# A hybrid decoder step on one core: retention's masked products one chunk later, one product for the new tokens' scores, the last group norm behind the next gate row, and token stores on ScalarE's queue

## Chip, cores and metric

One core of one Trainium2 chip runs the whole step as one program. The metric is device time in microseconds, from the host's view of one execution; the median of several runs counts. The profile is of one more execution, taken by the hardware profiler.

## What is computed

One step of a decoder layer for a prompt of 1024 tokens and for 8 sequences of 4 new tokens each, which have 1024 cached tokens behind them. Attention over the 256 best keys (chosen by an indexer) and retention (a linear recurrence in chunks of 128 tokens) run beside each other and are merged by gates. Of the reference, the parts that the change touches:

```python
def retention_chunk(state, q, k, v):
    ...
    scores = jnp.einsum('bihd,bjhd->bhij', q, k) * dmat
    out = jnp.einsum('bhij,bjhe->bihe', scores, v)
    ...
    out = out + jnp.einsum('bihd,bhde->bihe', q, state) * q_decay[None, :, :, None]
    ...
    new_state = (jnp.exp(lg * C)[None, :, None, None] * state
                 + jnp.einsum('bjhd,bjhe->bhde', k * k_decay[None, :, :, None], v))

def group_norm_heads(o):
    mu = jnp.mean(o, axis=-1, keepdims=True)
    var = jnp.mean(jnp.square(o - mu), axis=-1, keepdims=True)
    y = (o - mu) * lax.rsqrt(var + EPS)

def index_scores(qi, wi, ki):
    s = jnp.einsum('bqhd,bsd->bqhs', qi.astype(jnp.float32), ki.astype(jnp.float32))
    ...
    return jnp.einsum('bqhs,bqh->bqs', jax.nn.relu(s), w)
```

The step also returns the keys and values of all tokens, token by token.

## The kernel before

Activations are kept transposed, channels by tokens: 1056 tokens (1024 of the prompt, 32 new ones) in three chunks of 352 columns. A **row** of the projection is 128 output channels: for each chunk, 24 products of 128x128 weights (three terms for each of eight input tiles, lines 225 to 227) fill one PSUM bank `pj`, and ScalarE or VectorE copies the bank out. There are two such banks in the pool `psj`; while `third[0]` is set, every third chunk takes a bank `pj3` out of the retention's own pool. The weights of a row are loaded by SP (`ws`, L204), cast by ScalarE (`wh`, L210), and the remainder is subtracted by VectorE or GpSimd (`wl`, L211).

The program is written as one stream. A scheduler orders each engine's instructions by a timeline of its own, within the data's order and the `issue_after` limits that the code states; each engine then runs its list strictly in order. `last_on(engine)` is the last instruction that was written for an engine.

`retention` runs over four pairs of heads. For a pair, `pair` projects keys, queries, values and gates, rotates keys and queries, builds the eight chunk states (the scan L758, copied to `SD` by L760), and makes the scores (L766), which VectorE masks (L774). Between stands `rows`, a generator that projects a row of attention queries (`split_rows`): `next(rows)` makes one of its three chunks, casts it on ScalarE (L613) and subtracts the rest on VectorE (L616); after the third, four small copies take the new tokens' part (L619). After the first chunk come the state products (L784) and the masked-score products (L787), whose result is copied and transposed into `O` (L793 to L798). The group norm follows: mean on VectorE (L807, L808), centring on GpSimd (L810), Square on ScalarE (L812), variance and reciprocal root on VectorE (L814 to L817), scaling on GpSimd (L818), transposes on PE (L824). Then a gate row (`gates`, tanh on ScalarE, L880), the modulation's gate columns (`gate_rows`, products L218, copy L655, sum L659) and a second gate row.

In the last pair `new_tokens` runs ahead of the norm: scores of all new tokens' keys and queries (two products L847, one for each head, in two banks, masked by L851), output (L853), the products with the old states and the new states (L861, L863), the state update on VectorE (L867), and the old states' part of the output (L872 to L874). `third[0]` is cleared in it, because one of its banks is `pj3`.

VectorE has a second task over this stretch: the choice of the 256 best keys, whose passes (L1052 and lines up to 1135) fill its list; ScalarE counts signs for it (L1059).

Behind the retention come four key rows and four value rows. Each is turned into tokens (`to_tokens`, L678, copied to `tk` by L1179) and stored (L1181, L1183; the values once more to a scratch tensor, L1185). Between them stand the scores of the new queries against cached keys: SP loads gathered keys (`kv`, L1265), VectorE transposes them (`kt`, L1271), PE multiplies (L1250). SP issues in order, so a load stands behind a store that waits for its copy.

Early in the program the indexer's scores of the new tokens against cached keys pass through six ReLUs on ScalarE (L1026, L1028), then through the products L1032 on PE.

Of the kernel before, what the change touches and what calls it, by code (L numbers as in the profile page):

```python
# [8 lines left out]
F32 = mybir.dt.float32  # L9
# [4 lines left out]
OP = mybir.AluOpType  # L14
# [109 lines left out]
def _hybrid_step(ctx, tc, A, outs, dbg):  # L124
# [504 lines left out]
    def retention(gp):  # L629
        with ExitStack() as s3:  # L630
# [51 lines left out]
    def pair(rp, RC, O, SD, new, p, rows):  # L682
# [31 lines left out]
        for x, t in ((KN, kT), (QN, qT)):  # L714
            nc.gpsimd.tensor_copy(x[:, p], t[:, T:])
# [62 lines left out]

        end = next(rows)
# [21 lines left out]
        if p == 3:  # L801
            new_tokens(rp, RC, O, new, rows, vtok[:, 8], kd[:, 8])

        n, n8 = (18, 9) if p == 3 else (16, 8)
        o18 = O[:, :n8].rearrange("p t h e -> p (t h) e")
        mu = rp.tile([128, 18], F32, name="mu", bufs=1)[:, :n]
        nc.vector.tensor_reduce(mu, o18, op=OP.add, axis=AX.X)  # L807
        nc.vector.tensor_scalar(mu, mu, -1.0 / 64, None, op0=OP.mult)  # L808
        yc = o18
        nc.gpsimd.tensor_tensor(yc, o18, mu.unsqueeze(2).to_broadcast([128, n, 64]), op=OP.add)  # L810
        sq = big(rp, "tmp")[:, :n8].rearrange("p t (h e) -> p (t h) e", h=2)
        nc.scalar.activation(sq, yc, AF.Square)  # L812
        va = rp.tile([128, 18], F32, name="va", bufs=1)[:, :n]
        nc.vector.tensor_reduce(va, sq, op=OP.add, axis=AX.X)  # L814
        nc.vector.tensor_scalar(va, va, 1.0 / 64, EPS, op0=OP.mult, op1=OP.add)
        rs = rsqrt(rp, va, n, room=18)
        nc.vector.tensor_scalar(rs, rs, 0.5, None, op0=OP.mult)  # L817
        nc.gpsimd.tensor_tensor(yc, yc, rs.unsqueeze(2).to_broadcast([128, n, 64]), op=OP.mult)  # L818
        y2 = yc.rearrange("p (t h) e -> p t (h e)", h=2)
        yT = flat(big(rp, "tmp"))  # L820
        for g in (0, 1):
            p_ = pt()
            for j in range(4):
                nc.tensor.transpose(p_[:, 128 * j:128 * j + 128], y2[:, 4 * g + j], ident)  # L824
            sl = slice(512 * g, 512 * g + 512)
            normed[p] = nc.vector.scalar_tensor_tensor(yT[:, sl], p_, gT[:, p:p + 1], zsT[:, sl], op0=OP.mult, op1=OP.mult)
# [924 lines left out]
```

## Time and profile before

| | |
|---|---|
| time, median of 3 runs | 1049.01 us (1048.07 to 1051.84) |
| time of the profiled execution | 1049.86 us |
| its span, first to last instruction | 1048.2 us |
| mean granted clock of TensorE | 0.994 |
| ScalarE busy | 450.2 us |
| GpSimd busy | 223.9 us |
| DMA, mean over the span | 193 GB/s |

A profile names engines PE (matmul), PEld (weight load), DVE (VectorE), ACT (ScalarE), POOL (GpSimd) and SP (the queue that issues most transfers; SPq and ACTq mark the issuing of a transfer). Tiles are written `out<-in`. A row of a timeline gives start and duration in us, engine, line, operation, tiles, shape, and in brackets how long the engine stood idle before it and what ended that. A row of the waits gives engine, tile and line that waited, what ended the wait, us in total, times, and the longest.

### The profile page before, as it was taken

The page shows a single profiled execution, that of the slowest core. Times are in us where ns is not written, and L with a number is a line of the kernel's source. Part 1 is how long each engine was busy: PE and PEld are TensorE (multiplying, and loading weights), DVE is VectorE, ACT ScalarE, POOL GpSimd, SP SyncE. Part 2 cuts the span into 40 slices and gives each one's busy share as a digit, 9 for nine tenths or more (in the row PEclk, how much of TensorE's full clock was granted, in tenths as well). Part 3 has the DMA queues.
Part 4 walks back from the last instruction along what each step waited for, and adds up shares of the span by engine and source line. Part 5 has one row for each costly group of instructions (what it writes and reads, how often), then busy time and mean ns, then how long its engine had stood idle before and what let it go on. Part 6 is the DMA issues. An engine that isn't in the chain of part 4 may idle for free. (4 is left out here: it accounts for less than half of the span.)

```text
span 1048.2 us, 20021 instructions
## 1 busy us (share of the span) xinstructions
PE 1023.3 (98%) x7766; PEld 952.4 (91%) x7766; DVE 684.4 (65%) x1537; ACT 450.2 (43%) x926; POOL 223.9 (21%) x192
## 2 busy tenths in 40 slices
PE   7999999999999999999899999999999999999996
PEld 6899999999999999998799998778999999998776
DVE  6877369788977878989344443111367676586765
ACT  5685445554654555232233222122256576433111
POOL 0017436013320211120200021532033333000000
PEclk9999999999999999999899999999999999999998
DMA  9937676375445726664588788868867511656531
GB/s 303 282 81 198 190 224 176 104 225 155 143 150 165 194 63 221 173 144 144 172 307 291 262 261 299 285 217 297 276 228 232 203 68 32 210 178 224 186 106 61
DMA packets 183907, 202.53 MB, mean 193 GB/s; under 512 B 24308, under 2 KB 153348, under 8 KB 182724
## 3 DMA queue, kind: packets, MB, share of 16 engines
q1 hardware_dynamic: 171520, 175.07, 53.3%
q0 software_dynamic: 11776, 25.32, 7.6%
q8 instruction: 61, 1.00, 0.4%
q10 hardware_dynamic: 516, 0.86, 0.2%
q14 instruction: 34, 0.28, 0.1%
HBM read 156.11 MB, written 57.95 MB: 204 GB/s over the span
## 5 line engine op out<-in xcount | busy, mean ns | idle before, releaser
L225 PE MATMUL pj<-hh,wh 128*128 128x352 f32 (+1 forms) x1168 | 383.4, 328 | 1.1 <-ACT raw L880 0.8
L227 PE MATMUL pj<-hh,wl 128*128 128x352 f32 (+1 forms) x1168 | 377.2, 323 | 0.2 <-POOL wl L211 0.2
L226 PE MATMUL pj<-hl,wh 128*128 128x352 f32 (+1 forms) x1168 | 377.2, 323 | 0.0
L225 PEld LDWEIGHTS pj<-hh,wh 128*128 128x128 f32 x1168 | 219.9, 188 | 11.1 <-issue 6.8
L227 PEld LDWEIGHTS pj<-hh,wl 128*128 128x128 f32 x1168 | 219.9, 188 | 3.1 <-issue 2.5
L226 PEld LDWEIGHTS pj<-hl,wh 128*128 128x128 f32 x1168 | 220.3, 189 | 2.5 <-issue 2.1
L1052 DVE TENSOR_SCALAR_CACHE_REDUCE eq<-sc,cand 128x896 bf16<-128x896 f32 (+4 forms) x155 | 135.8, 876 | 2.8
L210 ACT CAST wh<-ws 128x1024 fp32r<-128x1024 f32 (+1 forms) x65 | 61.1, 941 | 125.6 <-PE pj L226 88.1
L211 POOL TENSOR_TENSOR wl<-ws,wh 128x1024 fp32r<-128x1024 f32 x18 | 43.7, 2428 | 224.4 <-ACT wh L210 224.2
L211 DVE TENSOR_TENSOR wl<-ws,wh 128x1024 fp32r<-128x1024 f32 (+1 forms) x47 | 54.5, 1161 | 47.1 <-ACT wh L210 47.0
L1436 POOL TENSOR_SCALAR lg<-lg,st 128x1024 f32<-128x1024 f32 (+7 forms) x64 | 47.3, 761 | 110.0 <-DVE st L1433 100.3
L1271 DVE STREAM_TRANSPOSE kt<-kv 128x1024 f32<-128x1024 f32 x32 | 38.7, 1234 | 43.5 <-DMA kv<-KG 43.2
L1428 ACT ACTIVATE lg<-lg,st 128x1024 f32<-128x1024 f32 (+7 forms) x64 | 49.5, 775 | 28.8 <-DVE st L1422 24.5
L1662 PE MATMUL pj<-woh,MH 128*128 128x512 f32 (+1 forms) x136 | 51.4, 378 | 0.0
L1663 PE MATMUL pj<-wol,MH 128*128 128x512 f32 (+1 forms) x136 | 51.2, 377 | 0.0
L1664 PE MATMUL pj<-woh,ML 128*128 128x512 f32 (+1 forms) x136 | 51.2, 377 | 0.0
L1241 POOL DMA_INDIRECT kv<-in_cache_v,idx x32 | 31.8, 994 | 57.8 <-PE sx L1305 40.2
L880 ACT ACTIVATE raw<-pj 128x352 f32<-128x352 f32 x48 | 21.8, 460 | 45.1 <-PE pj L227 42.5
L1679 ACT ACTIVATE u<-xo 128x512 f32<-128x512 f32 (+2 forms) x19 | 11.6, 609 | 67.0 <-DVE xo L1678 42.9
L1059 ACT ACTIVATE ra<-sc,cand 128x1024 bf16<-128x1024 f32 x31 | 35.6, 1149 | 6.2 <-DVE cand L1135 5.6
L1059 ACT ACTIVATE ra<-scs,cand 32x1056 bf16<-32x1056 f32 x31 | 36.4, 1175 | 0.8
L1422 DVE CUSTOM_DVE_ANT_0 lg<-x,bi 128x512 f32<-128x512 f32 (+3 forms) x64 | 35.3, 570 | 1.5 <-PE x L1421 1.1
(389 smaller groups left out, 1837.2 us busy)
## 6 DMA issues: line engine op xcount, KB each, us to landing
ws<-in_w_in SPq DMA_DIRECT2D x49, 512.0 KB
kv<-KG SPq DMA_DIRECT2D x32, 512.0 KB
KG<-in_cache_k SPq DMA_DIRECT2D x40, 256.0 KB
rot<-in_rot SPq DMA_DIRECT2D x8, 1056.0 KB
x<-in_w_ada SPq DMA_DIRECT2D x16, 512.0 KB
TG<-raw SPq DMA_DIRECT2D x15, 528.0 KB
KG<-in_cache_k POOLq DMA_DIRECT2D x24, 256.0 KB, 8.0
wst<-in_w_out SPq DMA_DIRECT2D x12, 512.0 KB
```

The costliest lines, as they stand in the source:

```text
L210: nc.scalar.copy(wh[:, :, :n], ws[:, :, :n])
L211: (nc.vector if k == 4 or len(order) % 3 else nc.gpsimd).tensor_sub(wl[:, :, :n], ws[:, :, :n], f32(wh[:, :, :n]))
L225: nc.tensor.matmul(p, wh[:, k], HH[k][:, sl], start=(k == 0), stop=False)
L226: nc.tensor.matmul(p, wh[:, k], HL[k][:, sl], start=False, stop=False)
L227: nc.tensor.matmul(p, wl[:, k], HH[k][:, sl], start=False, stop=(k == KT - 1))
L1052: nc.vector.tensor_scalar(junk[:n, :W], sc, thr[:n, j:j + 1], 0.0, op0=op, op1=OP.add, accum_out=cnt[:n, j:j + 1])
L1059: nc.scalar.activation(junk[:n, :W], sc, AF.Sign, bias=thr[:n, NV + j:NV + j + 1], scale=-1.0, accum_out=cnt[:n, NV + j:NV + j + 1])
L1428: nc.scalar.activation(l, l, AF.Exp, bias=st[:, i, 1:2], scale=-1.0, accum_out=st[:, i, 3:4])
L1436: nc.gpsimd.tensor_scalar(l, l, st[:, i, 2:3], 0.5, op0=OP.mult, op1=OP.mult)
L1662: nc.tensor.matmul(x, MH[:, k, tk], wh[:, k], start=(k == 0), stop=False)
L1663: nc.tensor.matmul(x, MH[:, k, tk], wl[:, k], start=False, stop=False)
L1664: nc.tensor.matmul(x, ML[:, k, tk], wh[:, k], start=False, stop=(k == KT - 1))
```

## The change

Six edits:

1. In `pair`, one more `next(rows)` stands ahead of the state products and the masked-score products: they come after the second query chunk.
2. `new_tokens` makes the scores of both heads as one product of 128 by 256 columns: the queries' tile is now zero where the other head's channels are (a memset once, two copies of 64 rows in place of one of 128). One bank, one mask operation.
3. `pair` gives its group norm back as a function, and for the last pair `new_tokens` also its second half, `states_of_new`. The caller runs that half behind the first chunk of the next gate row and the norm behind the whole of that gate row, its Square held behind the last tanh.
4. `third[0]` is cleared ahead of the last query chunk and set again behind the norm, so that `gate_rows` and the second gate row of the last pair have three banks.
5. Of the six ReLUs, VectorE makes the three of the first group.
6. The token stores are issued by ScalarE's queue, not by SP's.

```diff
-            new = [rp.tile([128, 4, NS], F32, name=n + "s4") for n in "kqvz"]
+            new = [rp.tile([128, 4, NS], F32, name=n + "s4") for n in "kvz"]
+            new.insert(1, rp.tile([128, 2, 4, NS], F32, name="qs4"))
+            nc.gpsimd.memset(new[1], 0.0)
...
-                pair(rp, RC, O, SD, new, p, rows)
+                norm = pair(rp, RC, O, SD, new, p, rows)
+                if p < 3:
+                    norm()
+                if p == 3:
+                    third[0] = None
                 for _ in rows:
                     pass
-                gates(gp, (4 + 2 * p,))
+                for c, end in enumerate(gate_parts(gp, (4 + 2 * p,))):
+                    if p == 3 and c == 0:
+                        states_of_new, norm = norm
+                        states_of_new(end)
+                if p == 3:
+                    norm(last_on(mybir.EngineType.Activation))
+                    third[0] = ps
                 summed = gate_rows(rp, p)
...
-        for x, t in ((KN, kT), (QN, qT)):
-            nc.gpsimd.tensor_copy(x[:, p], t[:, T:])
+        nc.gpsimd.tensor_copy(KN[:, p], kT[:, T:])
+        for i in (0, 1):
+            nc.gpsimd.tensor_copy(QN[head[i], i, p], qT[head[i], T:])
...
+        next(rows)
         end = next(rows)
 
         po = two()
...
+        def norm(behind=None):
...
+            with ExitStack() as held:
+                if behind:
+                    held.enter_context(tc.issue_after(behind))
+                nc.scalar.activation(sq, yc, AF.Square)
...
-        px = apart()
-        together([lambda i=i: nc.tensor.matmul(px[i][:, :128], KN[head[i]].rearrange("p q t -> p (q t)"),
-                                               QN[head[i]].rearrange("p q t -> p (q t)"), start=True, stop=True) for i in (1, 0)])
-        ss = rp.tile([128, 2, 128], F32, name="ss")
-        for i in (0, 1):
-            nc.vector.tensor_tensor(ss[:, i], px[i][:, :128], RC[:, R_MS + 128 * i:R_MS + 128 * i + 128], op=OP.mult)
+        px = ps.tile([128, 512], F32, name="pb", bufs=3)[:, :256]
+        nc.tensor.matmul(px, KN.rearrange("p q t -> p (q t)"), QN.rearrange("p i q t -> p (i q t)"), start=True, stop=True)
+        ss = big(rp, "tmp").rearrange("p t c -> p (t c)")[:, :256]
+        nc.vector.tensor_tensor(ss, px, RC[:, R_MS:R_MS + 256], op=OP.mult)
...
-        next(rows)
-        third[0] = None
-        end = next(rows)
-        po, pn = two(), [pt(), pt()] + apart()
-        with tc.issue_after(end):
+        def states_of_new(end):
+            po, pn = two(), [pt(), pt()] + apart()
+            with tc.issue_after(end):
...
+            def positive(G, out, x):
+                if G:
+                    nc.scalar.activation(out, x, AF.Relu)
+                else:
+                    nc.vector.tensor_scalar(out, x, 0.0, None, op0=OP.max)
...
-                nc.sync.dma_start(out_p[0, 0, 128 * t0:128 * t0 + 512, 2 * p:2 * p + 2].rearrange("(t p) h d -> p t (h d)", p=128), tk)
+                nc.scalar.dma_start(out_p[0, 0, 128 * t0:128 * t0 + 512, 2 * p:2 * p + 2].rearrange("(t p) h d -> p t (h d)", p=128), tk)
```

(The two other token stores change in the same way.)

How the lists of the engines move, at three places. Each row is a line of the kernel, the operation, tiles, the shape written, and a count; line numbers of after are some 12 to 28 higher.

ScalarE at the end of the retention, before: the last cast of the query row, its four small copies, the gate row's three tanhs with the Square among them, and the copy of the gate columns.

```order
L613 CAST raw<-pj 128x352
L619 COPY qs<-pj 32x32 x4
L880 ACTIVATE raw<-pj 128x352
L812 ACTIVATE tmp<-O 128x1152
L880 ACTIVATE raw<-pj 128x352 x2
L655 COPY zt<-pj 128x256
```

The same place after:

```order
L613 CAST raw<-pj 128x352
L619 COPY qs<-pj 32x32 x4
L902 ACTIVATE raw<-pj 128x352 x3
L830 ACTIVATE tmp<-O 128x1152
L667 COPY zt<-pj_5618 128x256
```

The Square (now L830) has moved behind the second and third tanh (now L902).

ScalarE in the third pair, from the copies of the chunk states on, before:

```order
L760 COPY SD<-S 64x8x64 x2
L613 CAST raw<-pj 128x352
L1059 ACTIVATE ra,cnt<-sc_761,cand 128x1024
L1059 ACTIVATE ra,cnt<-scs,cand 32x1056
L793 COPY tmp<-pb 128x512 x2
L798 COPY O<-pt 128x512 x2
L613 CAST raw<-pj 128x352
```

The same after (L1087 counts signs, L807 and L812 copy the products' result):

```order
L773 COPY SD<-S 64x8x64 x2
L613 CAST raw<-pj 128x352
L1087 ACTIVATE ra,cnt<-sc_761,cand 128x1024
L1087 ACTIVATE ra,cnt<-scs,cand 32x1056
L613 CAST raw<-pj 128x352
L807 COPY tmp<-pb 128x512 x2
L812 COPY O<-pt 128x512 x2
```

The second chunk's cast now stands ahead of the copies of the masked-score products; on PE 24 projection products have moved ahead of the state products.

SP in the first two key rows, before: key loads, weights, the row's own stores to scratch (`kd`), and the token stores.

```order
L1265 DMA kv<-KG 128x1024 x4
L204 DMA ws<-in_w_in 128x8x128
L623 DMA kd<-raw 128x1024
L1181 DMA out<-tk 128x4x128
L623 DMA kd<-raw 128x1024
L204 DMA ws<-in_w_in 128x8x128
L1181 DMA out<-tk 128x4x128
L1183 DMA out<-tk 32x128
L1265 DMA kv<-KG 128x1024 x4
```

The same after:

```order
L1293 DMA kv<-KG 128x1024 x4
L204 DMA ws<-in_w_in 128x8x128
L623 DMA kd<-raw 128x1024 x2
L1293 DMA kv<-KG 128x1024 x4
L204 DMA ws<-in_w_in 128x8x128
```

ScalarE around the first key row's second store and the next row's first chunks, after, with the counters that each row waits for (a transfer takes the next of eight counters, DMAHW0 to 7, and waits until the last user of that counter has landed):

```order
L1207 COPY tk<-pt 128x512 [waits PE_49]
L1207 COPY tk<-pt 32x128 [waits DMAHW3_49,PE_49]
L615 COPY kx<-pj 128x352 [waits Activation_49]
L1209 DMA out<-tk 128x4x128 [waits DMAHW2_49,Activation_49]
L1211 DMA out<-tk 32x128 [waits DMAHW4_49,Activation_49]
L613 CAST raw<-pj 128x352 [waits PE_49]
```

The stores (now L1209 and L1211) have left SP's list for ScalarE's, ahead of the next chunk's cast.

More of the change, by code (lines that the diff above doesn't have):

```diff
@@ L801, in pair @@
         if p == 3:
[L802 to L826, printed above, removed]
-        nc.sync.dma_start(YR[128 * p:128 * p + 128, :T], yT[:, :T])
@@ L835, in new_tokens @@
+        return norm if p < 3 else (states_of_new, norm)
+    def new_tokens(rp, RC, O, new, vt, kt):
         KN, QN, VN, ZN = new
@@ L866, in new_tokens @@
-        for q in (3, 2, 1, 0):
-            nc.vector.scalar_tensor_tensor(ST0[:, q], ST0[:, q], RC[:, R_GS + q:R_GS + q + 1], pn[q], op0=OP.mult, op1=OP.add)
-            nc.sync.dma_start(sts_out[0, :, 2 * q:2 * q + 2].rearrange("b h d e -> (h d) b e"), by_batch(q))
-        whole = big(rp, "tmp").rearrange("p t c -> p (t c)")
-        t, t8 = whole[:, :1024].rearrange("p (i b e) -> p i b e", i=2, b=NB), whole[:, 1024:]
-        for i in (0, 1):
-            nc.vector.tensor_tensor(t[:, i], po[i].rearrange("p (b e) -> p b e", b=NB), own, op=OP.mult)
@@ L873, in new_tokens @@
-        nc.vector.tensor_reduce(t8.rearrange("p (h e) -> p h e", h=2), t.rearrange("p i b e -> p i e b"), op=OP.add, axis=AX.X)
-        nc.vector.tensor_tensor(o8, o8, t8, op=OP.add)
+        def states_of_new(end):
+            po, pn = two(), [pt(), pt()] + apart()
+            with tc.issue_after(end):
+                together([lambda q=q, i=i: nc.tensor.matmul(po[i][32 * q:32 * q + 32], QN[head[i], i, q], ST0[head[i], q], start=True, stop=True)
+                          for q in range(4) for i in (0, 1)] +
+                         [lambda q=q, i=i: nc.tensor.matmul(pn[q][head[i]], kt[32 * q:32 * q + 32, head[i]],
+                                                            vm[32 * q:32 * q + 32, i].rearrange("p b e -> p (b e)"), start=True, stop=True)
+                          for q in range(4) for i in (0, 1)])
+            for q in (3, 2, 1, 0):
+                nc.vector.scalar_tensor_tensor(ST0[:, q], ST0[:, q], RC[:, R_GS + q:R_GS + q + 1], pn[q], op0=OP.mult, op1=OP.add)
+                nc.sync.dma_start(sts_out[0, :, 2 * q:2 * q + 2].rearrange("b h d e -> (h d) b e"), by_batch(q))
+            whole = big(rp, "tmp").rearrange("p t c -> p (t c)")
+            t, t8 = whole[:, :1024].rearrange("p (i b e) -> p i b e", i=2, b=NB), whole[:, 1024:]
+            for i in (0, 1):
+                nc.vector.tensor_tensor(t[:, i], po[i].rearrange("p (b e) -> p b e", b=NB), own, op=OP.mult)
+            nc.vector.tensor_reduce(t8.rearrange("p (h e) -> p h e", h=2), t.rearrange("p i b e -> p i e b"), op=OP.add, axis=AX.X)
+            nc.vector.tensor_tensor(o8, o8, t8, op=OP.add)
```

60 lines of the change are left out of this document (41 added, 19 removed).

## The prediction

> **What bounds the kernel now.** I read the page's engine table first, then the list of what each engine waited for (TensorE, PE, alone), then a table of stretches for the clock, and last the timelines of the stretches that these point at.
>
> The page's first row, and the list of PE's waits (engine, tile and line, what released it, us in total, times, longest):
>
> ```profile
> PE 1023.3 (98%) x7766; PEld 952.4 (91%) x7766; DVE 684.4 (65%) x1537; ACT 450.2 (43%) x926; POOL 223.9 (21%) x192
> PE pj L218 <- ACT raw L880: 3.5, 1, 3.5
> PE sx L1250 <- DVE kt L1271: 1.6, 1, 1.6
> PE pb L784 <- ACT SD L760: 1.5, 1, 1.5
> PE pj L847 <- DVE raw L616: 1.2, 1, 1.2
> PE pt L1032 <- ACT rl L1028: 0.9, 1, 0.9
> PE pj L225 <- ACT raw L880: 0.8, 1, 0.8
> ```
>
> PE is busy 98% of the span, and matmuls follow each other without gaps in most of it. So the time is the sum of PE's products plus its few waits, and an edit is worth what it takes from that list. All six waits quoted stand beside code that the change touches: together 9.5 us.
>
> The stretches (busy time of PE, PEld, DVE, ACT, POOL, then the granted clock, DMA share, GB/s) show one more price:
>
> ```profile
> 500.00:505.00 5.00, 1.51 (x18) 1.19 (x21) 1.45 (x3) 1.87 (x3) 2.12 (x1) 0.82 0.34 82
> 505.00:510.00 5.00, 5.00 (x41) 4.55 (x34) 2.71 (x14) 0.75 (x2) 1.69 (x1) 0.50 0.72 220
> 510.00:515.00 5.00, 5.00 (x35) 4.98 (x35) 1.41 (x2) 1.13 (x2) 2.82 (x2) 1.00 0.44 123
> ```
>
> After the 3.5 us wait the granted clock is 0.50, for about 5 us, and then 1.00 again. PE counts as fully busy there, at half speed.
>
> **Step 1, the group norm behind the gate row.** PE, ACT and POOL around the wait (start, duration, [idle before, releaser]):
>
> ```profile
> 500.71 2.12 POOL L810 TENSOR_TENSOR O<-O,mu 128x1152 f32<-128x1152 f32 x1 [30.69 <-DVE mu L808]
> 502.86 1.16 ACT L812 ACTIVATE tmp<-O 128x1152 f32<-128x1152 f32 x1 [9.39 <-POOL O L810]
> 503.93 0.80 ACT L880 ACTIVATE raw<-pj 128x352 f32<-128x352 f32 x2
> 504.43 1.93 PE L218 MATMUL pj<-ws,scT 128*32 128x128 f32 x32 [3.49 <-ACT raw L880]
> 403.14 1.08 PE L218 MATMUL pj<-ws,scT 128*32 128x128 f32 x32
> 506.29 0.66 PE L225 MATMUL pj<-hh,wh 128*128 128x352 f32 x1
> 509.98 0.34 PE L225 MATMUL pj<-hh,wh 128*128 128x352 f32 x1
> ```
>
> ACT's Square sat idle 9.39 us for POOL's centring, with two gate tanhs queued behind it, and these hold the two PSUM banks that the next products need. With the Square behind the third tanh, the tanhs run when their chunks end. Worth: the wait, 3.49; the same L218 group at full clock took 1.08 against 1.93 (0.85); and the 12 products from 506.29 to 509.98 took 3.69, against half of that at clock 1.00 (1.8). Sum 6.1 us. What is late next is DVE, because the gate-row products then want the third bank, which the state update leaves last:
>
> ```profile
> 491.70 0.52 DVE L616 TENSOR_TENSOR raw<-pj,raw 128x352 fp32r<-128x352 f32 x1
> 493.03 0.43 PE L225 MATMUL pj<-hh,wh 128*128 128x352 f32 x1 [0.28 <-ACT qs L619]
> 498.00 0.74 DVE L867 SCALAR_TENSOR_TENSOR rot<-rot,rc,pj 128x512 f32<-128x512 f32 x1
> 498.66 0.28 DVE L874 TENSOR_TENSOR O<-O,tmp 128x128 f32<-128x128 f32 x1
> ```
>
> DVE runs without a gap from the masks to 500.5, with the selection's last passes, and that work only changes places. So L616 of the third query chunk still ends near 492.2 and its bank still comes free near 493.0, which PE's next gate chunk awaits in both orders. PE reaches that point earlier now (its 1.16 us wait at L847 is gone, the states' products have moved behind one gate chunk) and waits longer there. I therefore book **nothing** for the 1.2 and 0.3 us rows. From 493.03, two chunks end at 504.43 - 3.49 = 500.94. DVE, which now does the 0.28 us add ahead of its last state update, has freed the bank by 499.0 to 499.4. Margin some 1.5 us. Behind the waiting Square stand now the copy of the gate-row sums and the cast of the next weights; PE has three chunks of products before it needs either, 11.9 us (the two chunks from 493.03 to 500.94 make 3.95 each, 0.165 a product).
>
> Here the Trainium skill has a rule beside the row: "TensorE: Matmul & The Clock Gate", Part 1: The HAM clock gate, says that the clock falls to half after about 3.4 us of idleness and comes back after about as long under load. The trace agrees (half after 3.49 us, full after the waits of 1.5 and 1.6); by the rule a wait of 2 us left over would still save the 2.6 us of slow clock.
>
> **Step 2, masked-score products a chunk later.** PE, ACT and DVE in the third pair:
>
> ```profile
> 373.32 1.89 DVE L1066 TENSOR_SCALAR inc<-cnt 128x5 int32<-128x5 f32 x1
> 376.87 2.32 ACT L760 COPY SD<-S 64x512 f32<-64x512 f32 x2 [3.45 <-DVE S L758]
> 379.25 1.83 PE L784 MATMUL pb<-qrT,SD 128*128 128x128 f32 x14 [1.48 <-ACT SD L760]
> 405.99 1.94 POOL L818 TENSOR_TENSOR O<-O,rs_y 128x1024 f32<-128x1024 f32 x1 [14.45 <-DVE base L1133]
> 411.73 0.71 PE L824 MATMUL pt<-C,O 128*128 128x128 f32 x5
> ```
>
> A second chunk (3.95 us) now covers the chain of scan and copy: **1.5** us gone. The price: the norm starts a chunk later, while its transposes (L824) come earlier in PE's order, seen from the attention products: 149 projection products between in place of 167. The slack between POOL's end (407.93) and PE's start (411.73), 3.8 us, shrinks by 18 x 0.165 = 3.0. Still covered, at nothing; without that cover up to 2 us a pair in two pairs.
>
> **Step 3, scores of the new tokens as one product.** It writes one bank where there were two.
>
> ```profile
> 476.93 0.37 PE L847 MATMUL pj<-qs,ks 64*128 64x128 f32 x1 [1.16 <-DVE raw L616]
> ```
>
> The pair of 64-row products, side by side, took 0.37 for a first pass and nearly as long for a second, some 0.5 us; seven 128x128 products at L784 (the 379.25 row) took 1.83, so one of 256 columns 0.52. Difference within 0.1; zero. The added copy and memset on POOL (21% busy) and one 256-wide mask in place of two 128-wide ones on DVE: nothing.
>
> **Step 4, ReLUs on two engines.**
>
> ```profile
> 128.30 1.17 ACT L1028 ACTIVATE rl<-pl 128x512 f32<-128x512 f32 x1
> 130.32 2.12 ACT L1028 ACTIVATE rl<-pl 128x512 f32<-128x512 f32 x2
> 132.50 1.07 PE L1032 MATMUL pt<-rl,wsel 128*32 128x256 f32 x16 [0.85 <-ACT rl L1028]
> 133.63 1.71 DVE L1036 COPY scs<-pt 32x256 f32<-32x256 f32 x4 [8.95 <-PE pt L1032]
> ```
>
> DVE is idle 8.95 us there; three of ACT's six go to it, and ACT's end moves from 132.4 to about 130.8. PE arrives three products (0.5 us) earlier, at 131.2, and still finds it done: **0.85** (0.4 if ACT is a little slower).
>
> **Step 5, third bank back for the last gate row.** The 0.8 us row at L225 is a wait for a bank of that row; with three banks it goes: **0.8**.
>
> **Step 6, token stores on ACT's queue.**
>
> ```profile
> L1271 DVE STREAM_TRANSPOSE kt<-kv 128x1024 f32<-128x1024 f32 x32 | 38.7, 1234 | 43.5 <-DMA kv<-KG 43.2
> SPq L1181 <- ACT tk L1179: 26.6, 11, 6.9
> 539.79 0.58 SPq L1183 DMA_DIRECT2D out<-tk  x1
> 540.48 0.88 SPq L1265 DMA_DIRECT2D kv<-KG  x2
> 545.26 1.25 DVE L1271 STREAM_TRANSPOSE kt<-kv 128x1024 f32<-128x1024 f32 x1 [3.98 <-DMA kv<-KG]
> 642.34 1.93 PE L1250 MATMUL sx<-kt,QB 128*32 128x256 f32 x32 [1.57 <-DVE kt L1271]
> 522.31 0.27 ACTq L661 DMA_DIRECT2D GD<-zt  x1
> 526.62 0.46 ACT L615 COPY kx<-pj 128x352 f32<-128x352 f32 x1
> ```
>
> SP stood 26.6 us behind stores that waited for ACT's copies, and the key loads went out right behind them (540.48 after 539.79). Without them SP runs ahead, seven key loads in a row by the last stage, and DVE's transposes wait less for data. I take the whole **1.57** of the last product (bounds 0 and 1.57; DVE's waits for these loads total 43 us and only this one reached PE). ACT pays 36 issues of 0.27 (its own row) to 0.58 (SP's) each, 10 to 21 us over the eight key and value rows, on an engine that is busy 43% of the span: hidden. Against it stands a new wait: the first key row's five transposes now follow its second chunk at once, and the third needs that chunk's copy (a cast and L615's 0.46 behind it): **+0.75**, an estimate. The first key loads stand on SP behind the norm's two stores, and the norm now ends a gate row later in PE's order; the products that use them stand 20 products (3.3 us) later as well. I book nothing; up to 2 us if they are late.
>
> The Trainium skill speaks against this step: "DMA: Bandwidth & Descriptors", Issuing engines are not separate DMA queues, says that transfers from all issuing engines share the same 16 DMA engines. By it alone the step saves only issue time; the row of 26.6 us shows head-of-line waits instead, and without the step the sum is 1.57 smaller.
>
> **Sum.** 6.1 + 1.5 + 0.85 + 0.8 + 1.57 - 0.75 = 10.1 us off the profiled execution's 1049.86 (span 1048.2), 1039.8. That execution lies 0.85 above the median 1049.01, so against the median 1038.9; I say **1039.0**.
>
> **Rivals.**
> - *DVE sets the end of the retention* (15%): its chain ends over 1.5 us later than I read, and PE waits for the third bank in place of the tanh. For it: DVE has no gap there. It keeps the slow-clock gain, loses up to 3.5 us: 1041 to 1043.
> - *The stores only change queues* (15%): the last wait stays (+1.6), the norms' slack fails in a pair or two (+2 to 4): 1041 to 1045.
> - *ACT held up by its own queue* (7%), the slower side. A store on ACT waits for the landing of a transfer issued eight before, often a key load, and behind it stand the copies that free PSUM. A key load took 4.8 us from issue to use (540.48 to 545.26). A chunk is 3.8 us and there are two banks, so ACT may be about 2.5 us late for nothing; from there every us is PE's. If loads land in 8 us (4.8 was the first of four), the excess in each of the 8 rows is 8 - 4.8, some 3 us: 24 - 10 = 14 us lost, 1063. It decides from 1.3 us a row, where the gain is eaten.
> - *No effect* (3%): the scheduler's order is on paper only, and DVE's pace sets all: 1047 to 1049.
>
> **How the numbers follow.** My own case has 60% (1036 to 1041). Range 1035 to 1046: it leaves out most of the last two rivals. A measurement of this kernel tells 0.5%, 5.2 us, from no change. Faster by over 0.5% (under 1043.8): 0.60 + 0.15 + 0.06 = 0.81. Within: 0.09 + 0.03 + 0.02 = 0.14. Slower: 0.05.
>
> **What would show it.** Step 1: no wait at the gate-row products, clock 1.00 throughout the retention's end, their 32 products in 1.1 us; wrong if PE waits there for DVE. Steps 2 and 4: no waits at the state product and the index sums. Step 6: key loads issued further ahead of the transposes, the transposes' waits below 43 us; wrong if ACT's queue shows waits for landings of over 3 us and PE's projections wait for ACT. The prediction fails as a whole if new PE waits, in any place, exceed 5 us.

## The result, and the profile after

The changed kernel takes 1041.21 us (median of 6 runs, 1040.81 to 1043.05), the kernel before 1049.80 us beside it (6 runs). The ratio is 0.9921, interval 0.9907 to 0.9935: faster by 0.65 to 0.93%. The profiled execution is one of 1041.09 us with a span of 1039.1, so 8.8 us below the profiled one of before (1049.86). Forecast were 1039.0 us and a gain of 10.1 us.

PE's list of waits after the change (columns as in the prediction: what waited, what released it, us in total, times, longest):

```profile
PE pj L225 <- ACT qs L619: 1.2, 1, 1.2
PE pb L871 <- DVE tmp L869: 0.8, 1, 0.8
PE pt L690 <- ACT kx L615: 0.7, 1, 0.7
PE pj L225 <- DVE raw L616: 0.5, 1, 0.5
```

The six waits of before (9.5 us) are off the list. Beside the waits for input loads and rows of 0.2 us, four others stand there, 3.2 us. The stretches of 5 us around the place where the clock had been 0.50, and the timeline of the retention's end:

```profile
500.00:505.00 5.00, 5.00 (x32) 5.00 (x32) 2.69 (x9) 2.20 (x3) 0.80 (x1) 1.00 0.79 240
505.00:510.00 5.00, 5.00 (x33) 5.00 (x32) 3.06 (x6) 1.10 (x3) 4.04 (x2) 1.00 0.57 160
```

```profile
482.64 0.66 PE L871 MATMUL pb<-vtok,tmp 128*128 128x64 f32 x4 [0.80 <-DVE tmp L869]
489.70 0.52 DVE L616 TENSOR_TENSOR raw<-pj,raw 128x352 fp32r<-128x352 f32 x1
490.24 0.74 ACT L619 COPY qs<-pj 32x32 f32<-32x32 f32 x4 [4.93 <-DVE raw L616]
491.04 0.43 PE L225 MATMUL pj<-hh,wh 128*128 128x352 f32 x1 [1.16 <-ACT qs L619]
496.32 0.74 DVE L883 SCALAR_TENSOR_TENSOR rot<-rot,rc,pj 128x512 f32<-128x512 f32 x1
499.03 0.47 ACT L902 ACTIVATE raw<-pj 128x352 f32<-128x352 f32 x1 [3.38 <-PE pj L227]
500.83 1.17 ACT L830 ACTIVATE tmp<-O 128x1152 f32<-128x1152 f32 x1 [1.34 <-POOL O L825]
498.92 1.08 PE L218 MATMUL pj<-ws,scT 128*32 128x128 f32 x32
```

The Square (L830) now stands behind the third tanh (499.03), the products of the gate columns (L218, the "ada products" of some expectations) start without a wait and take 1.08 us in place of 1.93, and the clock is 1.00 throughout. VectorE has freed the third bank by 497.1, 1.9 us before PE wants it. In its place stands the wait of 1.16 at the bank of the third query chunk, behind L616 and four copies.

In the key rows the load-bound transposes and the new waits of PE:

```profile
L1299 DVE STREAM_TRANSPOSE kt<-kv 128x1024 f32<-128x1024 f32 x32 | 38.8, 1231 | 23.8 <-DMA kv<-KG 15.0 <-PE sx L1278 8.6
ACT tk L1207 <- DMA VD<-tk: 8.0, 4, 3.5
ACT tk L1207 <- DMA out<-tk: 1.2, 2, 0.8
```

VectorE's wait ahead of the key transposes fell from 43.5 to 23.8 us, and the last key product waits no more. ScalarE now stands 9.2 us for the landing of its own stores, up to 3.5 at a time: its copies wait until a buffer `tk` has been stored. PE's list shows no wait behind these.

**PE's lead at matched products.** Medians of four to six runs here scatter by 1 us, so the sums below are read from the traces. PE runs the same 3528 projection products of 352 columns (3504 at L225 to L227, 24 of the first rows at L241) in every kernel. The lead of a kernel is the start of the nth of them in the profile of before, less its start in that kernel's profile, less the same difference at product 100 (the input loads ahead of it differ by up to 1.7 us from run to run). Worked out in this way, in us:

| run | 400: behind the index sums | 1800: behind the third pair | 2400: in the first key row | 2700: behind the four key rows | 3000: behind the last key product | last |
|---|---|---|---|---|---|---|
| changed kernel | 0.97 | 2.44 | 8.87 | 6.96 | 8.62 | 8.96 |
| hold_off | 0.96 | 2.44 | 5.18 | 5.19 | 6.82 | 7.16 |
| norm_at_once | 0.96 | 2.31 | 3.80 | 2.72 | 4.34 | 4.68 |
| stores_on_sp | 0.96 | 2.36 | 9.33 | 7.20 | 7.45 | 7.79 |
| one_chunk | 0.97 | 1.33 | 8.22 | 6.74 | 8.40 | 8.73 |
| turn_late | 0.97 | 2.44 | 9.45 | 7.79 | 9.43 | 9.77 |
| wl_on_pool | 0.94 | 2.41 | 8.28 | 5.47 | 7.13 | 7.47 |
| two_scores | 0.97 | 2.44 | 9.37 | 7.41 | 9.07 | 9.33 |
| third_bank_off | 0.96 | 1.96 | 8.39 | 8.41 | 10.10 | 10.44 |
| relu_one | 0.10 | 1.51 | 8.50 | 6.73 | 8.06 | 7.83 |
| copies_first | 0.94 | 2.48 | 8.40 | 5.33 | 6.96 | 6.75 |
| last_pair_one | 0.95 | 2.28 | 8.66 | 7.34 | 9.03 | 8.80 |
| own_values_late | 0.94 | 2.48 | 9.44 | 7.13 | 8.77 | 8.58 |

One profile stands behind each row. stores_on_sp and turn_late are the changed kernel up to product 2400 (its siblings, below) and lead there by 9.33 and 9.45, the changed kernel by 8.87: the profile of the changed kernel has 0.80 at the mask (L871), most of the others 0.4 to 0.5. So differences under 0.6 us at 2400 and behind it are scatter. The lead also moves when other products change places with the nth one. In the kernel before, the last transpose of the group norm (L830, 0.27 us at 515.67) stands ahead of product 2400 (526.1); in the changed kernel it (L848, 518.05) stands behind product 2400 (517.1). So 0.3 us of its lead at 2400, and of what it seems to lose in the key rows, is order and not time. The same holds in every row but hold_off, norm_at_once and the four versions without the third bank (third_bank_off and the last three).

### The profile page after: what moved, and what is told of

It is laid out like the page before. It is cut to its first block, busy times and chain, and to the rows that moved or that the text cites. A ratio compares the mean times of both kernels' runs of the same rounds, so it can differ in the third digit from the quotient of the medians.

```text
span 1039.1 us, 20016 instructions
## 1 busy us (share of the span) xinstructions
PE 1020.2 (98%) x7764; PEld 949.6 (91%) x7764; DVE 693.3 (67%) x1539; ACT 449.2 (43%) x923; POOL 224.1 (22%) x197
## 5 line engine op out<-in xcount | busy, mean ns | idle before, releaser
L225 PE MATMUL pj<-hh,wh 128*128 128x352 f32 (+1 forms) x1168 | 382.6, 328 | 1.7 <-ACT qs L619 1.2
L227 PE MATMUL pj<-hh,wl 128*128 128x352 f32 (+1 forms) x1168 | 377.0, 323 | 0.2 <-POOL wl L211 0.2
L225 PEld LDWEIGHTS pj<-hh,wh 128*128 128x128 f32 x1168 | 219.2, 188 | 11.1 <-issue 6.6
L227 PEld LDWEIGHTS pj<-hh,wl 128*128 128x128 f32 x1168 | 219.3, 188 | 4.0 <-issue 3.3
L210 ACT CAST wh<-ws 128x1024 fp32r<-128x1024 f32 (+1 forms) x65 | 61.1, 942 | 116.7 <-PE pj L226 76.6
L1299 DVE STREAM_TRANSPOSE kt<-kv 128x1024 f32<-128x1024 f32 x32 | 38.8, 1231 | 23.8 <-DMA kv<-KG 15.0
L1707 ACT ACTIVATE u<-xo 128x512 f32<-128x512 f32 (+2 forms) x19 | 11.6, 609 | 67.2 <-DVE xo L1706 43.7
L902 ACT ACTIVATE raw<-pj 128x352 f32<-128x352 f32 x48 | 22.0, 460 | 42.4 <-PE pj L227 41.6
L1087 ACT ACTIVATE ra<-sc,cand 128x1024 bf16<-128x1024 f32 x31 | 35.6, 1149 | 6.4 <-DVE cand L1163 4.2
L1087 ACT ACTIVATE ra<-scs,cand 32x1056 bf16<-32x1056 f32 x31 | 36.4, 1174 | 0.8
```

What stands on the lines that cost most here:

```text
L210: nc.scalar.copy(wh[:, :, :n], ws[:, :, :n])
L225: nc.tensor.matmul(p, wh[:, k], HH[k][:, sl], start=(k == 0), stop=False)
L227: nc.tensor.matmul(p, wl[:, k], HH[k][:, sl], start=False, stop=(k == KT - 1))
L1087: nc.scalar.activation(junk[:n, :W], sc, AF.Sign, bias=thr[:n, NV + j:NV + j + 1], scale=-1.0, accum_out=cnt[:n, NV + j:NV + j + 1])
```

## The experiments

### The hold, and the place of the norm

`hold_off`:

```diff
-                    norm(last_on(mybir.EngineType.Activation))
+                    norm()
```

> The changed kernel without the hold: the Square of the last group norm is no longer kept behind the gate row's last tanh, everything else stays. ACT's order then has the Square right behind the row's first tanh. In the changed kernel the Square became ready at 500.8 us and ended at 502.0; the second tanh could run at 495.2. Theory 1 (the queue behind the Square makes the stall): the second and third tanh wait for the Square's end, PE finds no bank at the ada products of the gate row (498.9), and waits about 3.5 us there, released by a tanh; with the wait the granted clock falls to 0.50 for some 5 us, 2.6 us more. Sum +6, about 1047. Theory 2 (DVE sets this end, the order of the Square on ACT does not): the wait at these products stays below 1 us, the time within 1 us of 1041.2. For the clock: if the wait comes out at 3.0 us or less, the clock should stay 1.00 and the sum is the wait alone, +2 to +3.

1042.40 us, ratio 0.9941 (0.9924 to 0.9957). The stretches of 1 us and PE's row at the place:

```profile
499.00:500.00 1.00, 0.00 (x0) 0.00 (x0) 0.00 (x0) 0.83 (x1) 0.14 (x1) 1.00 0.00 0
501.00:502.00 1.00, 1.00 (x5) 1.00 (x5) 0.93 (x3) 0.30 (x2) 0.00 (x0) 0.57 0.13 55
503.00:504.00 1.00, 1.00 (x5) 1.00 (x4) 0.84 (x5) 0.00 (x0) 0.00 (x0) 0.50 0.93 250
504.00:505.00 1.00, 1.00 (x7) 1.00 (x6) 0.41 (x3) 0.00 (x0) 0.38 (x1) 0.72 1.14 346
```

```profile
497.17 1.08 PE L218 MATMUL pj<-ws,scT 128*32 128x128 f32 x32
499.17 1.16 ACT L830 ACTIVATE tmp<-O 128x1152 f32<-128x1152 f32 x1 [9.38 <-POOL O L825]
500.24 0.80 ACT L902 ACTIVATE raw<-pj 128x352 f32<-128x352 f32 x2
500.73 0.43 PE L225 MATMUL pj<-hh,wh 128*128 128x352 f32 x1 [2.48 <-ACT raw L902]
```

The mechanism is theory 1's: the Square idles 9.38 us on ScalarE, two tanhs stand behind it, PE waits for a tanh. The sizes are not. The products of the gate columns take the third bank, so the wait comes one group later and is 2.48 us. It slows the clock all the same, to 0.50 from about 501.1 to 504.6, against the last sentence of the expectation. At product 2400 the run is 3.7 us behind the changed kernel (5.18 against 8.87); it then loses nothing in the key rows, where the changed kernel loses 1.9, and ends 1.8 behind.

`norm_at_once`:

```diff
+                if p == 3:
+                    states_of_new, norm = norm
+                    states_of_new(next(rows))
+                    norm()
                 for _ in rows:
                     pass
-                for c, end in enumerate(gate_parts(gp, (4 + 2 * p,))):
-                    if p == 3 and c == 0:
-                        states_of_new, norm = norm
-                        states_of_new(end)
+                gates(gp, (4 + 2 * p,))
                 if p == 3:
-                    norm(last_on(mybir.EngineType.Activation))
                     third[0] = ps
```

> The changed kernel with the states of the new tokens and the whole group norm of the last pair written ahead of the gate row again (states behind the last query chunk), no hold. Theory 1 (the hold alone makes the gain, not where the states stand): ACT has the Square behind the first tanh again, so the same wait as without the hold, 3.5 us at the ada products and a slow clock behind it; +6, about 1047. Theory 2 (the position of the states is worth something by itself): the states a chunk earlier let DVE end its updates and POOL its centring up to 4 us earlier, the Square ends before PE needs a bank, and the time stays within 1.5 us of 1041.2.

1044.48 us, ratio 0.9956 (0.9940 to 0.9973). PE's waits that differ:

```profile
PE pj L225 <- ACT raw L902: 2.5, 1, 2.5
PE pt L842 <- POOL O L836: 1.2, 1, 1.2
PE pj L225 <- DVE raw L616: 0.9, 1, 0.9
```

The same tanh wait as without the hold, and a wait of the norm's transposes (L842), which now stand a gate chunk earlier on PE, for GpSimd's scaling. At 2400 the lead is 3.80, 5.1 less than the changed kernel's. So the hold is worth 3.7 us there and the place behind the gate row another 1.4; at the last product it is 1.8 and 2.5. Both theories miss the number; that the earlier states let GpSimd finish in time is refuted (the Square idles 9.37 us here too).

### The third bank

`third_bank_off`:

```diff
                     norm(last_on(mybir.EngineType.Activation))
-                    third[0] = ps
```

> The changed kernel without the third bank in the last gate row and its ada products. Theory 1 (the prediction): the wait of 0.8 us for a bank in the last gate row is back, +0.8. Theory 2 (the wait came from late tanhs, which the hold has mended): with two banks and tanhs that run at once no wait over 0.3 us appears in the last gate row; within 0.3 us over that stretch.

1039.74 us, ratio 0.9925 (0.9908 to 0.9941). Three of PE's waits:

```profile
PE pj L225 <- ACT qs L619: 1.1, 1, 1.1
PE pb L870 <- DVE tmp L868: 0.4, 1, 0.4
PE pj L225 <- ACT raw L901: 0.3, 1, 0.3
```

Theory 2's number holds: two banks cost 0.3 us in the last gate row, not 0.8. That the hold mended late tanhs is not shown. ScalarE in the kernel before, then in this run:

```profile
520.63 1.04 ACT L210 CAST wh<-ws 128x1024 fp32r<-128x1024 f32 x1 [3.22 <-PE pj L226]
521.59 0.46 ACT L880 ACTIVATE raw<-pj 128x352 f32<-128x352 f32 x1
510.95 1.05 ACT L210 CAST wh<-ws 128x1024 fp32r<-128x1024 f32 x1 [3.70 <-DMA ws<-in_w_in]
511.90 0.45 ACT L901 ACTIVATE raw<-pj 128x352 f32<-128x352 f32 x1
```

In both the tanh that PE awaits stands right behind a cast of the next weights, which itself had waited. The hold leaves this order as it is; how much the cast costs PE depends on when it starts.

The two waits in the key rows are gone as well. The lead stays at 8.4 from product 2400 to 2700, where the changed kernel falls from 8.87 to 6.96, and the trace ends 1.5 us ahead of it. The ratios of the two kernels (0.9925 and 0.9921) do not show this. The scheduler puts the first key row's five transposes in one piece behind that row's second chunk in the changed kernel (first fence, PE's order), and in pieces of two and three, a chunk apart, in this run (second fence, where the lines count one less):

```
L690 MATMUL pt<-C,kx 128x128 x5
```

```
L689 MATMUL pt<-C,kx 128x128 x2
L689 MATMUL pt<-C,kx 128x128 x3
```

The bank alone does not decide this. hold_off keeps it and has the pieces too, a chunk of 4 us apart and without a wait, and so has norm_at_once:

```profile
523.28 0.38 PE L690 MATMUL pt<-C,kx 128*128 128x128 f32 x2
527.32 0.49 PE L690 MATMUL pt<-C,kx 128*128 128x128 f32 x3
```

### The key rows

`turn_late`:

```diff
-        for c, _ in enumerate(split_rows(tl, O_KA + 128 * p, p, k_rows, ks, x)):
+        for c, end in enumerate(split_rows(tl, O_KA + 128 * p, p, k_rows, ks, x)):
...
-        token_rows(tl2, x, p, k_out, ks_out, None)
+        with ExitStack() as held:
+            if p == 0:
+                held.enter_context(tc.issue_after(end))
+            token_rows(tl2, x, p, k_out, ks_out, None)
```

> The changed kernel with the transposes of the first key row held behind that row's third chunk. In the changed kernel PE waits 0.7 us in the middle of them (with the break in the stream 0.84 us), and 0.5 us for a row's rest behind two key transposes at 570 us; the same products show neither wait in the run without the hold of the Square, which reaches them 2 us later. Theory 1 (each wait is a fault of order): the first wait goes, the second stays: -0.8 against the changed kernel from the start of the key rows on. Theory 2 (the landing of the key loads sets the pace of the key rows, PE's gain ahead of them is given back there): the 0.8 comes back as a longer wait at the second key row, and the key rows end within 0.3 us of the changed kernel's.

1039.32 us, ratio 0.9917 (0.9900 to 0.9933). (What the expectation calls the second key row, at 570 us, is the fourth.) The changed kernel's two rows, from its timeline, then what stands in PE's list of this run instead:

```profile
522.12 0.55 PE L690 MATMUL pt<-C,kx 128*128 128x128 f32 x3 [0.68 <-ACT kx L615]
570.77 0.43 PE L225 MATMUL pj<-hh,wh 128*128 128x352 f32 x1 [0.50 <-DVE raw L616]
```

```profile
PE pj L225 <- ACT ks L619: 0.5, 1, 0.5
PE pj L225 <- DVE raw L616: 0.3, 1, 0.3
```

The first wait goes and another comes at the end of the same row (0.5 us, for the copies of its last columns). The key rows lose 1.66 us (9.45 to 7.79) where the changed kernel loses 1.91. The trace ends 0.8 ahead of the changed kernel's, but 0.6 of that was there at 2400 already, ahead of the edit. Theory 2 comes closer in the sum: a gain carried into the key rows is partly lost there. Its cause is not shown, since the new wait is for ScalarE's copies and not for a key load.

`stores_on_sp`:

```diff
-                nc.scalar.dma_start(out_p[0, 0, 128 * t0:128 * t0 + 512, 2 * p:2 * p + 2]...
+                nc.sync.dma_start(out_p[0, 0, 128 * t0:128 * t0 + 512, 2 * p:2 * p + 2]...
```

(and so for the two other stores)

> The changed kernel with the token stores on SyncE's queue again, nothing else undone. Theory 1 (the prediction): the last key product waits for a transpose again, +1.6 us; the five transposes of the first key row stay where they are in PE's order, so their wait of 0.7 us stays; 1042.8. Theory 2 (from the trace of the changed kernel): the stores' gain is partly given back inside the key rows, since the earlier loads let a key transpose stand ahead of a row's rest on DVE (0.5 us at 570 us); then that wait goes when the stores go back, and the sum is +1.0, 1042.2. Theory 3 (the queue is worth nothing): the last wait had gone because PE's work shifted against the loads; within 0.5 us of 1041.2. In all three DVE's waits for the key loads go back from 24 us towards 43.

1041.08 us, ratio 0.9933 (0.9915 to 0.9951). PE's list:

```profile
PE sx L1278 <- DVE kt L1299: 1.4, 1, 1.4
PE pt L690 <- ACT kx L615: 0.7, 1, 0.7
PE pj L225 <- DVE raw L616: 0.5, 1, 0.5
```

The wait at the last key product is back. From product 2700 to 3000 the run gains 0.25 on the kernel before, the changed kernel 1.66: the stores' move is worth 1.4 us there. The waits of 0.7 and 0.5 are there with the stores on SP too, so they do not come from the stores' move. Theory 1 holds (1.4 at the place, 1.2 at the trace's end), though the medians, 0.1 apart, do not show it; the ratios (0.9933 and 0.9921, each to the kernel before beside it) differ by 1.3 us, within their intervals. VectorE's wait ahead of the key transposes is back at 36.9 us.

### The other edits

`one_chunk`:

```diff
-        next(rows)
         end = next(rows)
```

> The changed kernel with one query chunk in place of two between the scan of the states and the products with the states. Theory 1 (the prediction): the wait for the copy of the states in the third pair is back, +1.5 us, and nothing else changes: 1042.7. Theory 2 (the second chunk also took cover from the last pair): the last pair's wait for the masked new scores and for the third query chunk's bank (0.8 and 1.2 us) shrink by the same amount, and the time stays within 0.5 us of 1041.2.

1040.64 us, ratio 0.9932 (0.9910 to 0.9954). The wait for the states' copy in the third pair is back:

```profile
PE pb L797 <- ACT SD L773: 1.2, 1, 1.2
```

The lead at 1800 is 1.1 us smaller. In the last pair the three waits are 0.3, 0.6 and 0.4 us in place of 0.8 and 1.2. At 2400 the run is 0.65 behind the changed kernel and 1.1 to 1.2 behind its two siblings; at the end it is 0.2 behind the changed kernel and 1.0 behind turn_late. Theory 1 holds at the place; how much is left at the end lies within the scatter.

`two_scores` (the padded tile stays):

```diff
-        px = ps.tile([128, 512], F32, name="pb", bufs=3)[:, :256]
-        nc.tensor.matmul(px, KN.rearrange("p q t -> p (q t)"), QN.rearrange("p i q t -> p (i q t)"), start=True, stop=True)
+        px = apart()
+        together([lambda i=i: nc.tensor.matmul(px[i][:, :128], KN[head[i]].rearrange("p q t -> p (q t)"),
+                                               QN[head[i], i].rearrange("p q t -> p (q t)"), start=True, stop=True) for i in (1, 0)])
...
```

(and two masks in place of one)

> The changed kernel with the scores of the new tokens as two products of 64 rows in two banks again, and two masks. Theory 1 (the prediction: the one product is worth nothing): PE waits for the bank at the scores again (1.2 us in the kernel before), and waits that much less at the bank of the third query chunk (1.2 us in the changed kernel), since VectorE sets both; from the state products of the last pair to its end within 0.4 us of the changed kernel. Theory 2 (one bank in place of two takes a wait out of PE's way): the wait at the scores comes on top, +1.2 us.

1040.16 us, ratio 0.9927 (0.9910 to 0.9943). Neither theory has the waits right: PE does not wait at the scores in this run, and still waits 1.1 us at the bank of the third query chunk. The sum is theory 1's: leads of 9.37 at product 2400 and 9.33 at the last, where stores_on_sp and turn_late have 9.33 and 9.45 at 2400 and the changed kernel and turn_late 8.96 and 9.77 at the last. The one product is worth nothing that can be seen.

`relu_one`:

```diff
-                if G:
+                if True:
                     nc.scalar.activation(out, x, AF.Relu)
```

> The changed kernel with all six ReLUs of the index scores on ScalarE again. Theory 1 (the prediction): PE waits again for the last ReLU at the index sums, 0.85 us, and is later by this to the end: +0.9 against the changed kernel. Theory 2 (a gain ahead of the retention's end is taken back there, where VectorE sets a bank free): PE is 0.9 us later up to the last pair and within 0.3 us of the changed kernel behind it.

1041.85 us, ratio 0.9925 (0.9912 to 0.9938). PE waits 0.8 us for the last ReLU again. The lead is 0.10 at product 400 (0.97), 0.9 smaller at 1800, 0.95 smaller than turn_late's at 2400 and 1.1 smaller than the changed kernel's at the end: theory 1.

### VectorE's queue at the retention's end

`wl_on_pool`, for the weights of the last gate row alone:

```diff
-        (nc.vector if k == 4 or len(order) % 3 else nc.gpsimd).tensor_sub(...
+        (on or (nc.vector if k == 4 or len(order) % 3 else nc.gpsimd)).tensor_sub(...
```

> The changed kernel with one subtraction of 128x1024 for the weights of the last gate row on GpSimd in place of VectorE (1.20 us on VectorE at 488.05, 2.4 us on GpSimd elsewhere). It stands just ahead of the third query chunk's L616, whose bank PE awaits for 1.16 us. Theory 1 (the length of VectorE's queue sets the end of the retention): L616 ends 1.2 us earlier, PE's wait for the copies behind it falls below 0.3 us, 1.0 us gained. Theory 2 (a long GpSimd pass holds a VectorE instruction up: in the changed kernel a 128x18 product took 2.27 us beside one, 0.18 elsewhere): one of VectorE's passes beside it is stretched by 1 us or more, L616 is no earlier, the wait stays at 1.2 us or grows; within 0.5 us or slower.

1041.83 us, ratio 0.9945 (0.9929 to 0.9962). One VectorE pass in the changed kernel, then VectorE and GpSimd in this run, and PE's wait:

```profile
485.12 0.75 DVE L1135 SCALAR_TENSOR_TENSOR ra<-sc,base,ra 128x512 f32<-128x512 f32 x1
483.15 0.75 DVE L1134 SCALAR_TENSOR_TENSOR ra<-ra,rem,eq 128x512 f32<-128x512 f32 x1
483.94 2.88 DVE L1135 SCALAR_TENSOR_TENSOR ra<-sc,base,ra 128x512 f32<-128x512 f32 x1
483.88 2.40 POOL L211 TENSOR_TENSOR wl<-ws,wh 128x1024 fp32r<-128x1024 f32 x1 [17.12 <-ACT wh L210]
489.65 0.52 DVE L616 TENSOR_TENSOR raw<-pj,raw 128x352 fp32r<-128x352 f32 x1
490.99 0.43 PE L225 MATMUL pj<-hh,wh 128*128 128x352 f32 x1 [2.27 <-ACT qs L619]
```

Theory 2: a VectorE pass of 0.75 us (L1135), started 0.06 behind GpSimd's, took 2.88, and the wait grew from 1.16 to 2.27. The 1.2 us taken off VectorE came back as 2.1. (L616 stands at 489.65 here and at 489.70 in the changed kernel, but this trace is 0.84 us ahead at product 100 already, so L616 is 0.8 us later.) The Trainium skill, "SBUF — State Buffer", section SBUF: two separate sides, says that VectorE and GpSimd share one pair of ports as an exclusive lock, held for a whole instruction, by which a VectorE instruction with two SBUF inputs waits for the end of a GpSimd instruction that began first and reads SBUF. The trace agrees: 483.94 + 2.88 is 0.54 behind GpSimd's end at 486.28.

### Versions put together

`copies_first` (no third bank, and):

```diff
-            nc.vector.tensor_sub(hl[1][:, sl], y, f32(hl[0][:, sl]))
             if c == 2:
                 for k in range(4):
                     nc.scalar.copy(new[32 * p:32 * p + 32, k], y[32 * k:32 * k + 32, CH - NS:])
+            nc.vector.tensor_sub(hl[1][:, sl], y, f32(hl[0][:, sl]))
```

> The run without the third bank, with one thing more: ScalarE's copies of a query or key row's last 32 columns (0.74 us) stand ahead of VectorE's L616 on the same bank, no longer behind it. Theory 1 (the bank of the third query chunk is free only after L616 and then the copies): the wait of 1.13 us at that bank shrinks to 0.4 us, -0.7 against the run without the third bank, 1039.0. Theory 2 (VectorE's state updates behind it set the next bank): what goes there comes back as a wait of a gate chunk or the ada products; within 0.3 us of that run.

1041.92 us, ratio 0.9929 (0.9911 to 0.9948). The wait at the bank is 0.39 us, as theory 1 has it. But 1.6 us are lost at a tanh of the last gate row, and the key rows lose 3.1 (8.40 to 5.33). ScalarE and PE in the third key row:

```profile
541.34 0.40 ACTq L1208 DMA_DIRECT2D out<-tk  x1
552.94 0.25 ACT L1206 COPY tk<-pt 32x128 f32<-32x128 f32 x1 [8.94 <-DMA out<-tk]
554.27 0.46 ACT L615 COPY kx<-pj 128x352 f32<-128x352 f32 x1
554.78 0.55 PE L689 MATMUL pt<-C,kx 128*128 128x128 f32 x3 [1.71 <-ACT kx L615]
```

ScalarE stood 8.94 us for a store to land, 11.6 us after the issue of the one at 541.34, with a copy behind it that PE needed. That has the effect of the third rival of the prediction, in another kernel: with this order of ScalarE's queue a landing reaches PE. The wait itself is another one. The rival had a store wait for an earlier load; here a copy waits for one of the two buffers `tk`, whose store has not landed. The 1.6 us at the tanh stand behind the same weight cast as in third_bank_off (L210, from 510.46 to 511.50 here).

`last_pair_one` (copies_first, and):

```diff
-        next(rows)
+        if p < 3:
+            next(rows)
         end = next(rows)
```

> The run with the copies first and no third bank, and in the last pair one query chunk in place of two ahead of the products with the states (two in the other pairs). In the run with one chunk everywhere the wait in the third pair was back (1.23 us), the last pair's waits were 0.3, 0.6 and 0.4 us in place of 0.8 and 1.2. Theory 1: the third pair's wait stays away and the last pair gains 0.5 us, 1038.5. Theory 2 (VectorE paces the last pair in any order): within 0.3 us of the run with the copies first.

1040.78 us, ratio 0.9916 (0.9902 to 0.9930). The third pair's wait stays away. In the last pair 0.6 us stand at a query chunk and none at the gate row's first bank; a tanh in the last gate row costs 0.9 and the fourth key row's rest on VectorE 0.8. The trace ends 2.0 us ahead of copies_first and 1.6 behind third_bank_off: inconclusive.

`own_values_late` (copies_first, and the products L871 with their copy in a function that is called behind the last query chunk):

```diff
+        def own_values(end):
+            with tc.issue_after(end):
+                together([lambda i=i: nc.tensor.matmul(pi[:, head[i]], ss[:, 128 * i:128 * i + 128], vt[:, head[i]], start=True, stop=True) for i in (0, 1)])
+            nc.scalar.copy(o8, pi[:, :128])
...
```

> The run with the copies first and no third bank, and the products of the new tokens' masked scores with their values behind the last query chunk in place of some twenty products ahead of its end. Theory 1: PE's wait for the mask on VectorE (0.4 us) goes and nothing comes in its place, -0.4. Theory 2 (VectorE sets the bank of the third query chunk, PE only arrives earlier): the wait at that bank grows by the same 0.4 us; within 0.2 us.

1040.76 us, ratio 0.9912 (0.9897 to 0.9927). The wait at the mask is gone and the bank's wait did not grow (0.37 us): theory 1 at the place, 1.0 us of lead at 2400 over copies_first. The key rows take 2.3 us back, 1.1 of it at the transposes L690, which wait for ScalarE's copy.

No version is shown to be faster than the changed kernel: the intervals of turn_late, third_bank_off, last_pair_one and own_values_late all hold its 0.9921.

## Why the prediction was right, and where not

**The number.** 1041.2 us lies at the upper edge of the prediction's own case (1036 to 1041) and at the lower edge of two rivals (from 1041). The traces decide between them: PE does not wait for the third bank, no transpose of a norm waits, and the wait at the last key product is gone. So it is the own case, short by 1.5 us.

**Step 1, 6.1 us: right in mechanism, near in size.** Stall, slow group and slow clock are gone, as foreseen. From product 1800 to 2400 the changed kernel gains 6.4 us and its siblings 7.0, where steps 1, 3 and 5 were booked at 6.9. Against norm_at_once the changed kernel leads by 5.1 at 2400, 3.7 of them by the hold. (The 0.3 us of order named at the table is in the 6.4, the 7.0 and the 3.7.) The estimate that VectorE keeps a margin held (1.9 us, said 1.5). So did the booking of nothing for the waits of 1.2 and 0.3: 1.16 stands in their place, and a wait at the mask (0.8, and 0.3 to 0.5 in most other runs) that the prediction did not name.

**A side remark of step 1 is not safe.** By the rule that it took from the Trainium skill (some 3.4 us of idleness) a wait of 2 us was to leave the clock alone, and the trace of before was read as agreeing. A wait of 2.27 us (wl_on_pool) did leave it at 1.00, but waits of 2.48 us (hold_off) and 2.46 us (norm_at_once) slowed it, and in the kernel before the clock fell 2.2 us into the wait of 3.49 (last section).

**Step 2, 1.5 us:** 1.7 by the lead (0.73 at product 1600 to 2.44), 1.1 by taking it out. The norms' slack held in all pairs.

**Step 3, zero:** nothing that can be seen. **Step 4, 0.85:** 0.97 by the lead at product 400, 0.87 by taking it out.

**Step 5, +0.8: wrong.** The prediction read the 0.8 us at the last gate row as a lack of banks. The row that ended the wait was a tanh behind a weight cast of 1.04 us on ScalarE. Without the third bank the same order costs 0.3 us, and 0.9 to 1.6 us in copies_first, last_pair_one and own_values_late, where PE is 0.9 to 2.0 us further ahead at product 2328. So the bank hides a cost that depends on when PE and the cast arrive; no run puts the cast behind the tanh. Against that stands the scheduler's order in the key rows: the trace without the bank ends 1.5 us ahead, which the ratios do not show.

**Step 6, +1.57 - 0.75: both sizes right, one cause wrong.** Taking the stores' move back costs 1.4 us at the last key product. The five transposes in one piece cost a wait of 0.68, but not because of the stores: they stay in one piece with the stores on SP, and are in pieces with two banks, and with three banks in hold_off and norm_at_once. Which edit turns the scheduler's order is not shown. The 0.5 us at the fourth key row was not booked at all: two key transposes stand ahead of L616 on VectorE, one in the kernel before. third_bank_off has two there as well and no wait; its key load lands earlier (transpose at 564.97 in place of 567.61, in a trace that is 1.1 us ahead at product 100).

**The sum.** 10.1 booked, 8.96 in the lead, 8.6 between medians. The shortfall lies in the key rows, which give back 1.9 us of lead before the last product returns 1.66 (booked: +0.82, came: -0.25). In the changed kernel 1.2 of the 1.9 go between products 2400 and 2520, around the wait of 0.68, with the 0.3 of order among them, and 0.75 between 2640 and 2700, around the wait of 0.50. What fixes how much the key rows take back in other versions (0 to 3.1 us) stays open: the order of the transposes and the landing of loads and stores both move, and no run holds the order fixed while changing only the landing.

## What to carry to other kernels

Look at which instruction stands idle at the head of an in-order queue while others behind it hold buffers: moving it behind them was worth more here than any edit to the work itself. A wait for a buffer has to be priced after the edits ahead of it, since the same 0.8 us can be a late release and not a missing bank; look at what stands ahead of the releasing instruction in its own queue. Where a scheduler sets the order, every gain upstream reshuffles the stretches behind it, so read the changed order there, wait by wait, before booking the whole sum.

## What the hardware showed

The granted clock fell to 0.50 after less than 3 us of idleness. Two rows of the kernel before, in stretches of 1 us:

```profile
502.00:503.00 1.00, 0.00 (x0) 0.00 (x0) 0.00 (x0) 0.14 (x1) 0.83 (x1) 1.00 0.02 4
503.00:504.00 1.00, 0.00 (x0) 0.00 (x0) 0.00 (x0) 1.00 (x2) 0.00 (x0) 0.59 0.00 0
```

PE's last product there ends at 500.94, and a mean of 0.59 in the second stretch means 1.00 up to about 503.2 and 0.50 behind it: 2.2 us of idleness. In hold_off PE stood from 498.25 to 500.73, 2.48 us, and the clock fell at about 501.1, when it was running again. Ahead of both of the waits near 2.5 us stood 1.08 us of products with weights 32 columns wide; whether these count as full work is not shown. The waits of 1.57 (kernel before), 1.71 (copies_first) and 2.27 us (wl_on_pool, to 490.99) left the clock at 1.00:

```profile
490.00:492.00 2.00, 1.01 (x6) 1.01 (x7) 1.97 (x5) 1.16 (x5) 0.00 (x0) 1.00 0.52 209
492.00:494.00 2.00, 2.00 (x15) 2.00 (x14) 2.00 (x3) 0.00 (x0) 0.00 (x0) 1.00 1.04 291
```

So the length of the wait alone does not decide. The slow phase lasted some 3.4 us in hold_off, 6.8 in the kernel before (to 510.0). "TensorE: Matmul & The Clock Gate", Part 1: The HAM clock gate, in the Trainium skill gives one idle window of about 3.4 us for the fall and says that the window runs freely. The 2.2 and 2.48 us of idleness measured here lie below that, and the measurement decides.

A GpSimd pass lengthened a VectorE pass from 0.75 to 2.88 us (wl_on_pool), which here made work moved from VectorE to GpSimd dearer than its own time.
